# A layer's modulation from transposed weights: products summed along rows on VectorE, gates made into rows by diagonal blocks

## The chip, the cores and the metric

The kernel runs on one core of a Trainium2 chip. Its time is the device time of one execution in microseconds (us); of several runs the median counts. The engines are named TensorE (PE in the profile; PEld is its loading of weights), VectorE (DVE), ScalarE (ACT), GpSimd (POOL) and SyncE (SP), which here only issues DMA transfers.

## The reference

One layer of a decoder trunk over 256 positions of width 2048, all in fp32. What matters here is the modulation: six vectors of 2048 are computed from the conditioning vector `c`, and each half of the layer uses a shift, a scale and a gate.

```python
c_act = jax.nn.silu(c)                                       # (1, 2048)
mod = (c_act @ w_ada[l] + b_ada[l]).reshape(b, N_MOD, 1, d)  # w_ada: 2048 x 12288
shift1, scale1, gate1, shift2, scale2, gate2 = [mod[:, i] for i in range(N_MOD)]
h = rms_norm(x, norm_g[l, 0]) * (1.0 + scale1) + shift1
y = token_mixer(h, ...)             # w_in, three mixers, branch gates, w_out
x = x + gate1 * rms_norm(y, norm_g[l, 1])
h = rms_norm(x, norm_g[l, 2]) * (1.0 + scale2) + shift2
f = jnp.square(jax.nn.relu(h @ w_ff1[l])) @ w_ff2[l]
x = x + gate2 * rms_norm(f, norm_g[l, 3])
```

## The kernel before

**The large products.** h is kept transposed (channels on partitions) as a pair `hhi`, `hlo` whose sum is the fp32 value. Weights come in blocks of 1 MB or less into `raw` (three buffers); `split` (lines 176 to 185) turns a block of 1024 elements a partition into `whi` (a copy on ScalarE, line 183) and `wlo` (the difference on VectorE, line 184), and TensorE multiplies three times for each (lines 203 to 205). `whi` and `wlo` have three buffers each.

**Order of the program.** The start loads x and scales it by its rms, transposes it into `xnT`, and computes the first two columns of shift and scale. Then come five phases over the 16 column blocks of h, in groups of 2, 3, 4, 3 and 4 (`PH`, line 335): in each phase `modulate` (lines 323 to 332) makes h for the group from `a_col` and `t_col`, and 12 chunks of `w_in` are multiplied with it. The columns of the next group are computed between the chunks of a phase. After the phases come attention and the gates of the branches, mixed with one another, then the merge, `w_out`, the second norm, and last the feed-forward part (lines 904 to 931).

**The modulation.** `ada_gemv` (line 265) loads 1 MB or 768 KB of `w_ada` at a time, with its 2048 input rows on the partitions (16 blocks of 128), and adds the block times one column of `sil` (silu of c, a column per block) into `acc` on VectorE (line 281 for the first, line 283 for the rest). What is left is a sum over partitions. `ada_cols` (line 286) takes it on TensorE as matmuls of `acc` with a column of ones (line 292) and adds bias and gain on columns of 16 or fewer elements (lines 296 to 298). `ada_row` (line 300), for the gates, which are needed as rows on all partitions, takes it as matmuls of a matrix of ones with the split `acc` (lines 313, 314) and adds bias and gain (lines 315, 316), which two transfers broadcast from DRAM to all partitions.

**Queues and steps.** These generators are advanced step by step: in the phases by a count in the chunk loop (in the fourth phase, 1.2 steps a chunk, some go to the second half's columns, from `side["ada"]`), later by `fill`, once for each block of four `kt` in `gemm`, at the rate in `side["ada"][1]`. Until the fifth phase the modulation's blocks have three `raw` buffers of their own; from there on (`ring[:] = [st, 3]`, line 696) they share the three of the other weights. All weights are issued on SP's queue in program order: an issue that waits for its buffer holds up those behind it. Within an engine, instructions run in the order that the framework's scheduler gave them.

## Time and profile before

| | before |
|---|---|
| median of 3 runs | 1546.1 us (1539.91 to 1547.72) |
| profiled execution | 1540.46 us, of which 1537.8 us are the span from first to last instruction |
| TensorE busy | 1472.0 us (96%) |
| VectorE busy | 1072.6 us (70%) |
| ScalarE busy | 764.7 us (50%) |
| moved by DMA | 368.61 MB, 240 GB/s on the mean |

[...] In a row of a stretch stand its bounds, its length, the busy time (and the count of instructions) of PE, PEld, DVE, ACT and POOL, then PEclk, the DMA engines' busy share and what they moved. A row of the chain is a piece of the work that ended last: its start, its length and what it was. In a group of instructions the idle time stands in front of what ended it.

### The profile page before, as it was taken

Reading aid. Unit: us, or ns where it says so; the run is one execution under the profiler, and the core shown is the slowest. Engines: PE = TensorE matmul, PEld = TensorE weight load, DVE = VectorE, ACT = ScalarE, POOL = GpSimd, SP = SyncE. Lnnn points to the kernel's source line nnn. Section 1 sums busy time; section 2 is a strip of 40 time slices with the busy share of each in tenths; the row PEclk is TensorE's granted clock in tenths of the full one; section 3 lists DMA queues with packets and bytes.
Section 4 is the critical chain, followed back from the end, with each engine's and each line's share of the span. In section 5 each row is a group of like instructions: output and inputs, shape, how many; then the busy total and the mean of one; then the engine's idle time right before and its main releaser. Section 6 shows DMA issues by size and latency. Waiting matters only on the chain.

```text
span 1537.8 us, 17519 instructions
## 1 busy us (share of the span) xinstructions
PE 1472.0 (96%) x6635; PEld 1193.9 (78%) x6635; DVE 1072.6 (70%) x1358; ACT 764.7 (50%) x1089; POOL 30.0 (2%) x39
## 2 busy tenths in 40 slices
PE   3989999999999999999989999999999999999997
PEld 2768877887777668787867888888888888888886
DVE  6788898778887787779887556666655445454465
ACT  5644334653677765254456453345433544344542
POOL 1000001002000010000000000000000000000000
PEclk8999998998999999999999999999999999999999
DMA  9998988665566668888975667777676555566553
GB/s 321 316 330 302 324 309 302 212 200 180 197 232 212 223 222 316 298 295 294 338 257 174 215 240 246 228 251 241 220 243 216 184 190 191 192 192 192 184 195 113
DMA packets 182339, 368.61 MB, mean 240 GB/s; under 512 B 9722, under 2 KB 22272, under 8 KB 182000
## 3 DMA queue, kind: packets, MB, share of 16 engines
q1 hardware_dynamic: 180640, 363.30, 69.8%
q0 software_dynamic: 1616, 4.20, 0.9%
q8 instruction: 52, 0.85, 0.2%
q14 instruction: 31, 0.25, 0.0%
HBM read 365.38 MB, written 2.10 MB: 239 GB/s over the span
## 4 chain that ended last, share of the span: by engine, by line
PE 83%; DVE 7%; DMA 5%; ACT 2%; issue 1%; SPq 0%; DVEq 0%; ACTq 0%
PE ps_mm L204 25%; PE ps_mm L205 25%; PE ps_mm L203 25%; DVE wlo L184 3%; DVE acc L283 2%; PE ps_x L360 2%; DMA raw<-in_w_ada_dram 2%; ACT whi L183 1%; DMA raw<-in_w_in_dram 1%; PE ps_x L292 1%; DMA raw<-in_w_out_dram 1%; PE ps_x L637 1%; PE ps_x L671 1%; DMA x_h<-in_x_dram 1%; PE ps_pv L663 1%
## 5 line engine op out<-in xcount | busy, mean ns | idle before, releaser
L184 DVE TENSOR_TENSOR wlo<-raw,whi 128x1024 fp32r<-128x1024 f32 x484 | 577.1, 1199 | 373.3 <-ACT whi L183 372.2
L183 ACT ACTIVATE whi<-raw 128x1024 fp32r<-128x1024 f32 x484 | 499.6, 1037 | 606.2 <-PE ps_mm L205 510.7
L204 PE MATMUL ps_mm<-wlo,hhi 128*128 128x512 f32 x1260 | 500.7, 397 | 9.6 <-DVE wlo L184 9.6
L203 PE MATMUL ps_mm<-whi,hhi 128*128 128x512 f32 x1260 | 497.3, 398 | 9.2 <-ACT whi L183 6.1
L205 PE MATMUL ps_mm<-whi,hlo 128*128 128x512 f32 x1260 | 498.7, 396 | 0.0
L204 PEld LDWEIGHTS ps_mm<-wlo,hhi 128*128 128x128 f32 x1260 | 239.6, 190 | 66.3 <-DVE wlo L184 16.7
L203 PEld LDWEIGHTS ps_mm<-whi,hhi 128*128 128x128 f32 x1260 | 238.5, 190 | 61.8 <-ACT whi L183 8.2
L205 PEld LDWEIGHTS ps_mm<-whi,hlo 128*128 128x128 f32 x1260 | 239.3, 190 | 51.4 <-issue 1.9
L283 DVE SCALAR_TENSOR_TENSOR acc<-raw,sil,acc 128x1024 f32<-128x1024 f32 (+2 forms) x195 | 235.2, 1206 | 7.6 <-DMA raw<-in_w_ada_dram 5.3
L203 PE MATMUL ps_mm<-whi,fhi 128*128 128x512 f32 x496 | 193.3, 390 | 0.0
L205 PE MATMUL ps_mm<-whi,flo 128*128 128x512 f32 x496 | 193.0, 389 | 0.0
L204 PE MATMUL ps_mm<-wlo,fhi 128*128 128x512 f32 x496 | 193.0, 389 | 0.0
L205 PEld LDWEIGHTS ps_mm<-whi,flo 128*128 128x128 f32 x496 | 93.1, 188 | 19.3
L204 PEld LDWEIGHTS ps_mm<-wlo,fhi 128*128 128x128 f32 x496 | 93.1, 188 | 19.3
L203 PEld LDWEIGHTS ps_mm<-whi,fhi 128*128 128x128 f32 x496 | 93.1, 188 | 19.2
L643 ACT ACTIVATE e<-e,m 128x128 f32<-128x128 f32 (+1 forms) x64 | 28.3, 443 | 1.9 <-DVE m L640 1.9
L398 DVE TENSOR_TENSOR part<-part,ps_mm 128x512 f32<-128x512 f32 x40 | 25.9, 681 | 4.4 <-PE ps_mm L205 4.4
L909 ACT ACTIVATE r_t<-ps_mm 128x512 f32<-128x512 f32 x32 | 18.8, 589 | 15.7 <-PE ps_mm L205 15.7
L403 DVE TENSOR_TENSOR pl<-ps_x,ph 128x512 fp32r<-128x512 f32 (+1 forms) x32 | 20.9, 675 | 8.1 <-ACT ph L402 8.1
L653 ACT ACTIVATE e<-e,s 128x128 f32<-128x128 f32 (+1 forms) x64 | 23.1, 441 | 5.5 <-DVE s L650 5.5
L204 PE MATMUL ps_mm<-wlo,qe 128*128 128x512 f32 x64 | 25.0, 390 | 0.0
L203 PE MATMUL ps_mm<-whi,qe 128*128 128x512 f32 x64 | 24.9, 392 | 0.0
(283 smaller groups left out, 1060.3 us busy)
## 6 DMA issues: line engine op xcount, KB each, us to landing
raw<-in_w_ff_dram SPq DMA_DIRECT2D x128, 1024.0 KB, 5.2
raw<-in_w_in_dram SPq DMA_DIRECT2D x56, 1024.0 KB, 5.3
raw<-in_w_ada_dram SPq DMA_DIRECT2D x104, 512.0 KB, 5.5
raw<-in_w_ada_dram SPq DMA_DIRECT2D x32, 1024.0 KB, 5.1
raw<-in_w_in_dram SPq DMA_DIRECT2D x24, 768.0 KB, 5.9
raw<-in_w_out_dram SPq DMA_DIRECT2D x16, 1024.0 KB, 5.3
raw<-in_w_ada_dram SPq DMA_DIRECT2D x32, 384.0 KB, 5.8
raw<-in_w_br_nsa_dram SPq DMA_DIRECT2D x8, 1024.0 KB, 5.7
```

Source lines behind the costliest of these rows:

```text
L183: A.activation(hv, v, AF.Copy)
L184: V.tensor_sub(lv, v, hv.bitcast(F32))
L203: T.matmul(outs[t], ahi[:, kt, ts_], hv[:, k, c0:c0 + n], start=f, stop=False, skip_group_check=True)
L204: T.matmul(outs[t], ahi[:, kt, ts_], lv[:, k, c0:c0 + n], start=False, stop=False, skip_group_check=True)
L205: T.matmul(outs[t], alo[:, kt, ts_], hv[:, k, c0:c0 + n], start=False, stop=l, skip_group_check=True)
L283: V.scalar_tensor_tensor(acc, rv[:, :, k], sil[:, kt:kt + 1], acc, ALU.mult, ALU.add)
L360: T.transpose(tb[:, (k * NT + t) * P:(k * NT + t + 1) * P], src[t][:, (k2 * 2 + k) * P:(k2 * 2 + k + 1) * P], ident)
L398: V.tensor_add(d, d, ps)
L403: V.tensor_sub(lo, src, hi.bitcast(F32))
L643: A.activation(e[:, br, 0:L], e[:, br, 0:L], AF.Exp, scale=-1.0, bias=m8[:, hh, br:br + 1], accum_out=s8[:, hh, br:br + 1])
L653: A.activation(es[hh][:, br, 0:L], es[hh][:, br, 0:L], AF.Copy, scale=s8[:, hh, br:br + 1])
L909: A.activation(r_t[:, t], ps[t], AF.Relu)
```

## The change

The host lays `w_ada` out transposed (12288 rows of 2048), so that 128 outputs lie on the partitions and their 2048 inputs along a row; a block of 1 MB is then contiguous in DRAM. `sil` becomes a tile of 128 x 2048, c broadcast to all partitions, with silu computed on all of them (a factor of 0.5 is left to the product). `ada_col` loads a block and gives the 128 sums with one instruction of VectorE, product and sum along the row (`tensor_tensor_reduce`), in place. Nothing is left to sum over partitions. The gates are computed as columns too (`ada_gate`), bias and gain added there; the first gate stands ahead of the second half's columns in the queue of side work. `to_rows` makes rows of them: VectorE multiplies the identity with four columns at a time, giving four diagonal blocks of 128, which are split into two parts and multiplied with the matrix of ones; ScalarE copies the result. The broadcasts of the gates' bias and gain from DRAM go; their columns come through a third small transpose at the start (`rows2`).

```diff
-V_END = 160
+V_G1, V_G3, V_BG1, V_BG2 = 160, 176, 192, 208
+V_END = 224
...
-def trunk_kernel(ctx: ExitStack, tc: tile.TileContext, consts, x, c, norm_g, w_ada, b_ada, w_in,
+def trunk_kernel(ctx: ExitStack, tc: tile.TileContext, consts, w_adaT, x, c, norm_g, b_ada, w_in,
...
     cols = cp.tile([P, V_END], F32, name="cols")
-    sil = cp.tile([P, KT], F32, name="sil")
     a_col = cp.tile([P, KT], F32, name="a_col")
     t_col = cp.tile([P, KT], F32, name="t_col")
+    g1_col = cp.tile([P, KT], F32, name="g1_col")
+    g2_col = cp.tile([P, KT], F32, name="g2_col")
     a2_col = cp.tile([P, KT], F32, name="a2_col")
...
     ring = [pre, 3]
-    crow = pre.tile([KT, P], F32, name="crow")
     rows0 = pre.tile([96, P], F32, name="rows0")
     rows1 = pre.tile([64, P], F32, name="rows1")
-    nc.sync.dma_start(crow, c.rearrange("o (r p) -> (o r) p", p=P))
+    rows2 = pre.tile([64, P], F32, name="rows2")
+
+    sil = ad.tile([P, D], F32, name="sil")
+    for h in range(2):
+        hs = slice(h * 1024, (h + 1) * 1024)
+        nc.sync.dma_start(sil[:, hs], c[0, hs].partition_broadcast(P))
     nc.sync.dma_start(ident, consts[:, C_ID:C_ID + P])
...
         G.dma_start(rows1[k * KT:(k + 1) * KT], bav[sec])
-
-    tp0 = bank("x")
-    T.transpose(tp0[:, 0:KT], crow, ident[0:KT, 0:KT])
-    th = pre.tile([P, 2, KT], F32, name="th")
-    V.tensor_copy(th[:, 0], tp0[:, 0:KT])
-    A.activation(th[:, 1], tp0[:, 0:KT], AF.Tanh, scale=0.5)
-    V.tensor_scalar(th[:, 1], th[:, 1], 0.5, 0.5, ALU.mult, ALU.add)
-    V.tensor_mul(sil, th[:, 0], th[:, 1])
-    A.activation(th[:, 1, 0:1], th[:, 1, 0:1], AF.Sqrt)
+    for k, src in enumerate((norm_g[0, 1], norm_g[0, 3])):
+        G.dma_start(rows2[k * KT:(k + 1) * KT], src.rearrange("(r p) -> r p", p=P))
+    for k, sec in enumerate((2, 5)):
+        G.dma_start(rows2[(k + 2) * KT:(k + 3) * KT], bav[sec])
+
+    for h in range(2):
+        hs = slice(h * 1024, (h + 1) * 1024)
+        th = ring[0].tile([P, 2048], F32, name="raw", tag="raw", bufs=ring[1])[:, 0:1024]
+        A.activation(th, sil[:, hs], AF.Tanh, scale=0.5)
+        V.scalar_tensor_tensor(sil[:, hs], th, 1.0, sil[:, hs], ALU.add, ALU.mult)
+    warm = pre.tile([P, 1], F32, name="warm")
+    A.activation(warm, ident[:, 0:1], AF.Sqrt)
...
         T.transpose(tp1[:, 0:V_POS + 32], rows0[0:V_POS + 32], ident[0:V_POS + 32, 0:V_POS + 32])
-        T.transpose(tp1[:, V_BADA:V_END], rows1, ident[0:64, 0:64])
+        T.transpose(tp1[:, V_BADA:V_BADA + 64], rows1, ident[0:64, 0:64])
+        T.transpose(tp1[:, V_G1:V_END], rows2, ident[0:64, 0:64])
         V.tensor_copy(cols[:, 0:V_POS + 32], tp1[:, 0:V_POS + 32])
...
-    win_v, wada_v = kview(w_in), kview(w_ada)
+    win_v = kview(w_in)
     brp_v, brg_v, brn_v = kview(w_br_pool), kview(w_br_gmlp), kview(w_br_nsa)
...
-    def ada_gemv(c0, c1, acc):
-
-        n = acc.shape[2]
-        nk = 1024 // n
-        for u in range(0, KT, nk):
-            raw = ring[0].tile([P, 2048], F32, name="raw", tag="raw", bufs=ring[1])[:, 0:2 * nk * n]
-            if c1 == c0 + n:
-                rv = raw.rearrange("p (k s n) -> p s k n", k=nk, s=2)
-                nc.sync.dma_start(raw.rearrange("p (k n) -> p k n", k=nk), wada_v[:, u:u + nk, c0:c0 + 2 * n])
-            else:
-                rv = raw.rearrange("p (s k n) -> p s k n", k=nk, s=2)
-                for s_, c_ in enumerate((c0, c1)):
-                    nc.sync.dma_start(rv[:, s_], wada_v[:, u:u + nk, c_:c_ + n])
-            for k in range(nk):
-                kt = u + k
-                if kt == 0:
-                    V.tensor_scalar(acc, rv[:, :, k], sil[:, 0:1], None, ALU.mult)
-                else:
-                    V.scalar_tensor_tensor(acc, rv[:, :, k], sil[:, kt:kt + 1], acc, ALU.mult, ALU.add)
-            yield
+    def ada_col(col, sec, k):
+
+        raw = ring[0].tile([P, 2048], F32, name="raw", tag="raw", bufs=ring[1])
+        r0 = sec * D + k * P
+        nc.sync.dma_start(raw, w_adaT[r0:r0 + P, :])
+        V.tensor_tensor_reduce(raw, raw, sil, 0.5, 0.0, ALU.mult, ALU.add, accum_out=col)
...
-        acc = ad.tile([P, 1024], F32, name="acc", tag="acc", bufs=2)[:, 0:256 * nk]
-        yield from ada_gemv(sec * D + k0 * P, (sec + 1) * D + k0 * P, acc.rearrange("p (s n) -> p s n", s=2))
-        ps = bank("x")
-        for k in range(2 * nk):
-            T.matmul(ps[:, k:k + 1], acc[:, k * P:(k + 1) * P], ones[:, 0:1], start=k == 0, stop=k == 2 * nk - 1,
-                     skip_group_check=True)
+        for k in range(k0, k0 + nk):
+            for s_, c_ in enumerate((t_c, a_c)):
+                ada_col(c_[:, k:k + 1], sec + s_, k)
+                yield
         ks = slice(k0, k0 + nk)
         bs = V_BADA + vsec * KT + k0
-        V.tensor_add(a_c[:, ks], ps[:, nk:2 * nk], cols[:, bs + KT:bs + KT + nk])
+        V.tensor_add(a_c[:, ks], a_c[:, ks], cols[:, bs + KT:bs + KT + nk])
         V.scalar_tensor_tensor(a_c[:, ks], a_c[:, ks], 1.0, cols[:, vg + k0:vg + k0 + nk], ALU.add, ALU.mult)
-        V.tensor_add(t_c[:, ks], ps[:, 0:nk], cols[:, bs:bs + nk])
-
-    def ada_row(n, sec, gi, gg):
-
-        acc = ad.tile([P, 1024], F32, name="acc", tag="acc", bufs=2)
-        c0 = sec * D + n * 1024
-        gs = gg[:, n * 1024:(n + 1) * 1024]
-        nc.sync.dma_start(gs, b_ada[0, c0:c0 + 1024].partition_broadcast(P))
-        yield from ada_gemv(c0, c0 + 512, acc.rearrange("p (s n) -> p s n", s=2))
-        hv, lv = split(acc.rearrange("p (k n) -> p k n", k=2))
-        for b in range(2):
-            ps = bank("pv")
-            bs = slice(b * 512, (b + 1) * 512)
-            gb = ad.tile([P, 512], F32, name="gb", tag="gb", bufs=1)
-            nc.sync.dma_start(gb, norm_g[0, gi, n * 1024 + b * 512:n * 1024 + (b + 1) * 512].partition_broadcast(P))
-            T.matmul(ps, ones_r, hv[:, b], start=True, stop=False)
-            T.matmul(ps, ones_r, lv[:, b], start=False, stop=True)
-            V.tensor_add(gs[:, bs], gs[:, bs], ps)
-            V.tensor_mul(gs[:, bs], gs[:, bs], gb)
+        V.tensor_add(t_c[:, ks], t_c[:, ks], cols[:, bs:bs + nk])
+
+    def ada_gate(sec, vb, vg, g_c):
+
+        for k in range(KT):
+            ada_col(g_c[:, k:k + 1], sec, k)
+            yield
+        V.tensor_add(g_c, g_c, cols[:, vb:vb + KT])
+        V.tensor_mul(g_c, g_c, cols[:, vg:vg + KT])
+        gated.append(sec)
+
+    gated = []
+
+    def to_rows(g_c, gg):
+
+        for n in range(4):
+            dh, dl = (st.tile([P, 1024], F32R, name=t, tag=t, bufs=3)[:, 0:512] for t in ("whi", "wlo"))
+            d32 = st.tile([P, 2048], F32, name="raw", tag="raw", bufs=3)[:, 0:512]
+            V.tensor_tensor(d32.rearrange("p (k n) -> p k n", k=4), ident.unsqueeze(1).broadcast_to([P, 4, P]),
+                            g_c[:, 4 * n:4 * n + 4].unsqueeze(2).broadcast_to([P, 4, P]), ALU.mult)
+            A.activation(dh, d32, AF.Copy)
+            V.tensor_sub(dl, d32, dh.bitcast(F32))
+            ps = bank("x")
+            T.matmul(ps, ones_r, dh, start=True, stop=False)
+            T.matmul(ps, ones_r, dl, start=False, stop=True)
+            A.activation(gg[:, n * 512:(n + 1) * 512], ps, AF.Copy)
+            yield
...
     early_steps = []
+    side["ada"][0].append(ada_gate(2, V_BG1, V_G1, g1_col))
     for kc in range(4):
...
         if ph < NP - 1:
-            nxt, ns = [ada_cols(*PH[ph + 1], 0, 0, V_G0, a_col, t_col)], KT // (8 // PH[ph + 1][1])
+            nxt, ns = [ada_cols(*PH[ph + 1], 0, 0, V_G0, a_col, t_col)], 2 * PH[ph + 1][1]
         order = list(range(NE))[::1 - 2 * ((NP - 1 - ph) % 2)]
...
         T.matmul(pg[0:48, 0:S], lv[:, kt], hhi[:, kt], start=False, stop=kt == KT - 1)
-    gT = ad.tile([48, S], F32, name="gT", tag="gb", bufs=1)
+    gT = t0.tile([48, S], F32, name="gT")
     A.activation(gT, pg[0:48, 0:S], AF.Tanh, scale=0.5)
...
     gg1 = g1p.tile([P, D], F32, name="gg1")
-    rows = []
-
-    def row(n, *args):
-        yield from ada_row(n, *args)
-        rows.append(n)
-
-    side["ada"][0][1:1] = [row(n, 2, 1, gg1) for n in range(2)]
+    while 2 not in gated:
+        step(side["ada"][0])
+    side["rows"] = [[to_rows(g1_col, gg1)], 0.5, 0.0]
...
             ps = gemm_a_last(wout_v, n * 512, act, kept)
-        while n // 2 not in rows:
-            step(side["ada"][0])
+        drain("rows")
         for t in range(NT):
...
     gg2 = fl.tile([P, D], F32, name="gg2")
-    for n in range(2):
-        side["ada"][0].append(ada_row(n, 5, 3, gg2))
+    side["ada"][0] += [ada_gate(5, V_BG2, V_G3, g2_col), to_rows(g2_col, gg2)]
     side["ada"][1] = 0.25
...
-_INS = ['x', 'c', 'norm_g', 'w_ada', 'b_ada', 'w_in', 'pool_w', 'pool_scale', 'gmlp_ln_g', 'gmlp_ln_b',
+def _layouts(inputs):
+
+    import numpy as np
+    laid = {}
+    laid["w_adaT"] = np.ascontiguousarray(inputs["w_ada"][0].T)
+    return laid
+
+
+_INS = ['x', 'c', 'norm_g', 'b_ada', 'w_in', 'pool_w', 'pool_scale', 'gmlp_ln_g', 'gmlp_ln_b',
         'gmlp_ws', 'gmlp_bs', 'cmp_pos', 'cmp_w1', 'cmp_b1', 'cmp_w2', 'cmp_b2', 'w_br_pool', 'w_br_gmlp',
```

What stands in a row of an engine, before and after, at two places. The first is SP's queue at the start, before (`crow` is c as rows, `raw` a block of `w_ada`, `x_h` a half of 128 positions):

```order
L116 DMA crow<-in_c_dram 16x128
L117 DMA cst<-consts_dram 128x128
L277 DMA raw<-in_w_ada_dram 128x4x256 x2
L340 DMA x_h<-in_x_dram 128x1024 x4
L277 DMA raw<-in_w_ada_dram 128x4x256 x6
L173 DMA raw<-in_w_in_dram 128x2x512
```

and of the changed kernel:

```order
L122 DMA sil<-in_c_dram 128x1024 x2
L123 DMA cst<-consts_dram 128x128
L342 DMA x_h<-in_x_dram 128x1024 x2
L279 DMA raw<-in_w_adaT_dram 128x2048
L342 DMA x_h<-in_x_dram 128x1024 x2
L279 DMA raw<-in_w_adaT_dram 128x2048 x3
L183 DMA raw<-in_w_in_dram 128x2x512
```

The broadcast of c, 1 MB as it lands, now stands first, and a block of weights between the halves of x. The second place is VectorE from the end of x's scaling to the first columns of shift and scale, before:

```order
L283 SCALAR_TENSOR_TENSOR acc<-raw,sil,acc 128x512 x8
L148 COPY cols<-ps_x 128x71
L149 COPY cols<-ps_x 128x64
L283 SCALAR_TENSOR_TENSOR acc<-raw,sil,acc 128x512 x4
L184 TENSOR_TENSOR wlo<-raw,whi 128x1024
L296 TENSOR_TENSOR a_col<-ps_x,cols 128x2
L298 TENSOR_TENSOR t_col<-ps_x,cols 128x2
L297 SCALAR_TENSOR_TENSOR a_col<-a_col,cols 128x2
```

and of the changed kernel (ISA is `tensor_tensor_reduce`, its second row the reading of its accumulator):

```order
L280 ISA raw,t_col<-raw,sil 128x2048
L280 ISA t_col 128x1
L158 COPY cols<-ps_x 128x71
L159 COPY cols<-ps_x 128x128
L280 ISA raw,a_col<-raw,sil 128x2048
L280 ISA a_col 128x1
L292 TENSOR_TENSOR t_col<-t_col,cols 128x2
L290 TENSOR_TENSOR a_col<-a_col,cols 128x2
L194 TENSOR_TENSOR wlo<-raw,whi 128x1024
L291 SCALAR_TENSOR_TENSOR a_col<-a_col,cols 128x2
```

Between the two copies of `cols` and `a_col` four multiply-adds and a round through TensorE (line 292 of before) became one long instruction, and a `wlo` moved ahead of the last operation on `a_col`. In the loop of the phases the two multiply-adds of a step mostly stand together before, and one `ISA` pair takes their place.

## Rows read from the trace of the kernel before

**Rows 1.** The page, the chain that ended last: shares of the span by line.
```profile
PE ps_mm L204 25%; PE ps_mm L205 25%; PE ps_mm L203 25%; DVE wlo L184 3%; DVE acc L283 2%; PE ps_x L360 2%; DMA raw<-in_w_ada_dram 2%; ACT whi L183 1%; DMA raw<-in_w_in_dram 1%; PE ps_x L292 1%; DMA raw<-in_w_out_dram 1%; PE ps_x L637 1%; PE ps_x L671 1%; DMA x_h<-in_x_dram 1%; PE ps_pv L663 1%
```

**Rows 2.** Stretches: bounds, length, busy time of five engines, PEclk, DMA share, GB/s.
```profile
0.00:34.00 34.00, 9.98 (x46) 7.62 (x46) 20.65 (x43) 19.56 (x31) 6.54 (x17) 0.92 0.97 324
...
60.00:260.00 200.00, 189.02 (x826) 152.84 (x825) 175.73 (x205) 86.63 (x107) 0.00 (x0) 0.97 0.91 317
...
400.00:600.00 200.00, 199.11 (x877) 144.64 (x876) 163.31 (x320) 139.75 (x316) 7.08 (x4) 1.00 0.67 232
600.00:800.00 200.00, 194.02 (x861) 158.19 (x860) 162.27 (x173) 89.84 (x115) 0.00 (x0) 0.98 0.87 304
800.00:1538.00 738.00, 719.10 (x3241) 595.78 (x3239) 422.81 (x426) 339.18 (x399) 0.00 (x0) 0.99 0.62 206
```

**Rows 3.** The chain in order of time: start, length, what, xcount.
```profile
4.79 9.40 DMA x_h<-in_x_dram
...
28.24 1.65 PE ps_x L292 x8
...
63.90 1.25 PE ps_x L292 x12
...
120.06 1.92 PE ps_x L292 x16
189.67 1.23 PE ps_x L292 x12
...
232.31 2.23 PE ps_x L292 x16
...
397.19 1.68 PE ps_x L292 x16
...
619.15 5.27 DMA raw<-in_w_ada_dram
624.60 7.62 DMA raw<-in_w_in_dram
```

**Rows 4.** Line 283 by stretch: bounds, length, VectorE's busy time (xcount), PEclk, DMA.
```profile
60.00:260.00 200.00, 65.17 (x56) 0.97 0.91 317
...
400.00:600.00 200.00, 45.56 (x35) 1.00 0.67 232
600.00:800.00 200.00, 52.52 (x41) 0.98 0.87 304
```

**Rows 5.** Groups by form: line, engine, op, tiles, shapes, xcount, busy us, mean ns.
```profile
L283 DVE SCALAR_TENSOR_TENSOR acc<-raw,sil,acc 128x1024 f32<-128x1024 f32 x150 | 193.5, 1290 | 6.3 <-DMA raw<-in_w_ada_dram 4.8
...
L283 DVE SCALAR_TENSOR_TENSOR acc<-raw,sil,acc 128x768 f32<-128x768 f32 x30 | 30.4, 1014 | 0.3
...
L640 DVE CUSTOM_DVE_ANT_0 e<-ps_x,cst 128x256 f32<-128x256 f32 x32 | 11.8, 420 | 1.4 <-PE ps_x L637 1.3
L283 DVE SCALAR_TENSOR_TENSOR acc<-raw,sil,acc 128x512 f32<-128x512 f32 x15 | 11.3, 751 | 0.9 <-DMA raw<-in_w_ada_dram 0.4
...
L640 DVE CUSTOM_DVE_ANT_0 e<-ps_x,cst 128x128 f32<-128x128 f32 x32 | 7.8, 287 | 1.7 <-PE ps_x L637 1.5
...
L640 DVE DVE_READ_ACCUMULATOR2_ANT m<- 128x1 f32 x64 | 5.3, 83 | 0.0
```

**Rows 6.** Timeline before the first matmul: start, length, engine, line, op, tiles.
```profile
24.99 3.10 DVE L283 SCALAR_TENSOR_TENSOR acc<-raw,sil,acc 128x512 f32<-128x512 f32 x4
28.01 1.22 DVE L184 TENSOR_TENSOR wlo<-raw,whi 128x1024 fp32r<-128x1024 f32 x1
...
30.36 1.09 ACT L330 ACTIVATE h<-xnT,t_col,a_col 128x256 f32<-128x256 f32 x2 [4.51 <-DVE a_col L297]
...
32.30 0.61 ACT L331 ACTIVATE hhi<-h 128x512 fp32r<-128x512 f32 x1
```

**Rows 7.** DMA issues: tiles, queue, xcount, size of one, median us to landing.
```profile
gb<-in_norm_g_dram SPq DMA_DIRECT2D x8, 256.0 KB, 5.3
gg<-in_b_ada_dram SPq DMA_DIRECT2D x4, 512.0 KB, 6.3
```

More of the change, by code (lines that the diff above doesn't have):

```diff
@@ L984 @@
     args.append(nc.dram_tensor("consts_dram", cst.shape, _mybir.dt.float32, kind="ExternalInput").ap())
+    for name, a in _layouts(inputs).items():
+        arrays[f"in_{name}_dram"] = a
+        args.append(nc.dram_tensor(f"in_{name}_dram", a.shape, _mybir.dt.from_np(a.dtype), kind="ExternalInput").ap())
     for name in _INS:
```

## The prediction

> **What bounds the kernel now.** I read the chain first, then the stretches, then the chain again in order of time. The chain that ended last is TensorE's matmuls of lines 203 to 205 for three quarters of the span, VectorE's `wlo` and `acc` for 5%, transfers of weights for 4% [rows 1]. So the first question for every edit is whether it takes work off TensorE, and the second whether it moves one of the places where TensorE waits. The table of stretches shows those places [rows 2]. From 800 us on (most of it the feed-forward part, where TensorE is only idle at both ends) and from 400 to 600 us (attention and gates, 0.9 us idle) TensorE has no time to lose. Idle time stands in three places: the first 34 us (24 us idle: nothing can start before the first columns of h exist), 60 to 260 us (11 us idle), and 600 to 800 us (6 us idle). The reader should look at the other columns of these two rows. In 60 to 260 VectorE is busy for 175.7 of 200 us and the DMA engines for 0.91: both are near their end, and TensorE's 11 idle us come from them. In 600 to 800 the DMA share is 0.87, and the chain there runs through two transfers that TensorE stood waiting for, 5.3 and 7.6 us long [rows 3].
>
> The modulation's share of this: its multiply-adds take 65.2 us of VectorE's time in 60 to 260, 45.6 in 400 to 600 and 52.5 in 600 to 800 [rows 4], and the sums over partitions, one-column matmuls, stand on TensorE in nine short runs [rows 3].
>
> **Part by part, what is removed.** The nine runs of line 292 go. Their pieces of the chain are 1.65 us (start), 1.25, 1.92, 1.23 and 2.23 (60 to 260) and four of 1.68 (397, 490, 585 and 653 us; one is shown, the others read alike) [rows 3]: 15.0 us of a full TensorE. How much of it comes back depends on what ends last there, so I take them by stretch below. The partition sums of the gate rows (lines 313, 314) are replaced by as many matmuls of the same size on the diagonal blocks: 16 against 16, nothing.
>
> **VectorE.** Before, 1 MB of weights costs two multiply-adds of 1290 ns, 2.58 us (in the steps with 384 columns it is 768 elements, 1014 ns each, 16 for what is now six steps) [rows 5]. After, it costs one product-and-sum of 2048 elements, and no such instruction is in the trace. The nearest row is the same form in attention: 287 ns for 128 elements and 420 for 256 [rows 5], that is 1.04 ns an element, so 287 + 1920 x 1.04 = 2.28 us. Its accumulator read follows, 83 ns, which needs no more than that. The other bound is that the rate differs because both operands now lie in SBUF, where attention reads one from PSUM; the multiply-add, which reads two fp32 tiles from SBUF, gains 539 ns for 512 more elements, 1.05 ns each [rows 5], the same rate. I take 2.28. In 60 to 260 the loop's steps are 27 now (8, 6, 8 and about 5 early ones), 61.6 us against 65.2 of line 283 [rows 4] and a few first products on line 281 beside it: 4 to 6 us less on an engine that has 24 to spare there. What queues behind the long instruction is the next `wlo`, 2.28 us where it was 1.29; but two multiply-adds mostly stood together before (order, in the section on the change), so the block does not grow.
>
> **The start.** The last half of x lands at 14.19 us (4.79 + 9.40) [rows 3]. The last four multiply-adds begin at 24.99 and take 3.10; h begins at 30.36 and takes 1.09; `hhi` begins at 32.30, 0.85 us after h, with a `whi` between them [rows 6]. Now SP issues 1 MB of `sil`, then half of x, then 1 MB of weights, then the second half of x: ahead of the last half of x stand 1 MB more bytes than before. At the stretch's 324 GB/s [rows 2] that is 3.2 us, with the whole chain of rms, scaling, transposes and columns behind it; it is nothing if landing and not bandwidth sets the time. I take 2.9, near the upper end, since the DMA share is 0.97 there. Behind it: one product of 2.28 for the 3.10, no 1.65 us on TensorE, but in the new order a `wlo` (1.22 us [rows 6]) stands ahead of the last operation on `a_col`, and no `whi` stands between h and `hhi`. Sum: +2.9 - 0.8 - 1.65 + 1.2 - 0.85 = +0.8. Bounds: -2.1 without the first term, and +3. I take +1.
>
> **60 to 260 us.** 6.6 us of TensorE work go (1.25 + 1.92 + 1.23 + 2.23), VectorE loses 4 to 6, and 27 MB come in one issue a step in place of two, which I do not count as a gain. If VectorE alone set this stretch, it still shrinks by what VectorE loses; if all idle time went too, by 6.6 + 11 = 17.6. The low end, 3, is a stretch where only the sections without idle time pay (120 and 190 us). I take 8.
>
> **320 to 600 us.** Three runs of 1.68 us on a TensorE with no idle time between 400 and 600, and little before: 5.0 us, bounds 4 and 6.
>
> **600 to 800 us.** One run of 1.68 goes. The gate's bias and gain rows, broadcast to all partitions, go as well: half of 4 x 512 KB and 8 x 256 KB [rows 7] belongs here, 2 MB, at 304 GB/s [rows 2] 6.9 us of transfers in a stretch that waits for transfers. Against it, the four diagonal blocks of the first gate take one of three `raw` buffers each, and one `whi` and one `wlo`, on the way from product to copy to difference, behind other work of VectorE and ScalarE, while TensorE's next matmuls in order wait for them; a buffer out of use for some microseconds can bring a wait like one of the two in [rows 3] back. Between 0 and 9 us gained I take 5. The second gate's blocks lie after 800 us, where the DMA share is 0.62 and VectorE has 315 us to spare [rows 2]: nothing.
>
> **Sum.** +1 - 8 - 5 - 5 = -17 against the profiled execution's 1540.46 us (span 1537.8 and 2.7 around it): 1523.5. That execution lies 5.6 us under the median of the three runs and 0.5 above the lowest, so a median of a few runs may come as high as 1529. I forecast **1525**, and 1515 to 1533 for this case alone.
>
> **The rivals.** (a) *The sum along rows runs at half rate.* The operands are two fp32 tiles in SBUF, and an accumulator beside them; the trace has no such instruction. At 2.08 ns an element a step would take 4.41 us. 60 to 260 us: 27 steps cost 119 us, 51 more than now; VectorE then needs 227 us for what is done in 200, and at today's share (88%) 258, so 27 to 58 us longer; 400 to 600 (18 steps, 34 more): 0 to 41; 600 to 800 (21 steps, 40 more): 2 to 50. Less the 15 of TensorE that is 1555 to 1675, about 1615. It decides from some 2.9 us a step on: a step takes 2.5 now, and 27 x 0.4 eats the 10 us won elsewhere. Against it stands that line 283 reads two fp32 tiles from SBUF at 1.05 ns [rows 5].
>
> [...]
>
> (b) *The removed matmuls were in the shade.* Where VectorE or a transfer ends last, TensorE's 10 us outside attention turn into idle time, and the start loses 1: 1540.5 - 5 + 1 = 1536.5. For it speaks VectorE's 88%; against it that VectorE loses as much, and that most of 60 to 260 has TensorE at 189 of 200.
>
> (c) *The idle time goes too*: -2 (start), -17.6, -5, -9: 1507. For it speaks that two waits are for transfers that shrink; against it that the buffers, not bytes alone, set when a transfer starts.
>
> (d) *The diagonal blocks bring waits*: four like the two in [rows 3], 5.3 to 7.6 us each, are 21 to 30 us; with the other terms as they are 1540.5 + 1 - 8 - 5 - 2 + 26 = 1552. It decides from 14 us in all on. For it speaks that the stretch waits for transfers now; against it that the copies of `raw` wait for VectorE only briefly there (TensorE idles 6 us in 200).
>
> **How the numbers follow.** The forecast gets 0.62, (a) 0.08, (b) 0.15, (c) 0.10, (d) 0.05. Faster by over 0.5% (8 us, about what a measurement of this kernel can tell from no change) are the forecast nearly whole and (c): 0.73. Within 0.5% is (b) and the forecast's tail: 0.15. Slower: (a), (d): 0.12. The range reaches from (c) to (b) with the 5.6 us of the median on top, 1508 to 1542; it leaves out (a) and (d).
>
> **What would show it.** In the profile after: no one-column matmuls; the product-and-sum of 2048 elements at 2.2 to 2.4 us (at 4.4 rival (a) holds); the first matmul of line 213 at 32 to 36 us; VectorE's busy time some 20 us lower; 400 to 600 us of before done in 5 less; TensorE's idle time between 60 and 260 not above 11. I am wrong in size if the start slips by more than 3 us or if the stretch around the first diagonal blocks shows new waits of `ps_x` for VectorE; wrong in kind if VectorE comes out above 1100 us.

## The result, and the profile of the changed kernel

The changed kernel takes 1521.32 us (median of 4 runs, 1519.10 to 1524.53), the kernel before 1543.01 us beside it (4 runs, 1538.42 to 1547.72): a ratio of 0.9871, 95% interval 0.9846 to 0.9897, so 1.3% faster. The forecast was 1525.

First the page of the profiled execution (1522.03 us): its span, busy times and packets.

```profile
span 1519.7 us, 17069 instructions
PE 1451.0 (95%) x6507; PEld 1173.1 (77%) x6507; DVE 1052.1 (69%) x1341; ACT 770.4 (51%) x1102; POOL 36.4 (2%) x43
DMA packets 147074, 365.47 MB, mean 241 GB/s; under 512 B 8458, under 2 KB 8768, under 8 KB 134448
```

VectorE has 20.5 us less work than before (1072.6), TensorE 21.0 (1472.0). The groups of instructions show the new operations: the product-and-sum, its accumulator read, and the three steps of a diagonal block on VectorE and ScalarE (count | busy us, mean ns | idle before).

```profile
L280 DVE CUSTOM_DVE_ANT_0 raw<-raw,sil 128x2048 f32<-128x2048 f32 x96 | 219.2, 2286 | 9.3 <-DMA raw<-in_w_adaT_dram 9.3
L310 DVE TENSOR_TENSOR raw<-cst,g_col 128x512 f32<-128x512 f32 x8 | 5.5, 692 | 0.2
L313 DVE TENSOR_TENSOR wlo<-raw,whi 128x512 fp32r<-128x512 f32 x8 | 5.5, 691 | 4.7 <-ACT whi L312 4.7
L312 ACT ACTIVATE whi<-raw 128x512 fp32r<-128x512 f32 x8 | 5.1, 632 | 16.0 <-PE ps_mm L215 10.0 <-DVE t_col L292 6.0
L280 DVE DVE_READ_ACCUMULATOR2_ANT t_col<- 128x1 f32 x32 | 2.7, 84 | 0.0
```

The stretches, with the columns of [rows 2] (PEclk is the granted clock of TensorE as a share of its full clock):

```profile
60.00:260.00 200.00, 188.15 (x798) 150.36 (x797) 179.19 (x208) 89.56 (x110) 4.73 (x8) 0.98 0.90 334
400.00:600.00 200.00, 199.49 (x868) 146.12 (x867) 161.09 (x305) 139.14 (x311) 11.58 (x4) 1.00 0.70 245
600.00:800.00 200.00, 183.96 (x805) 147.79 (x804) 162.11 (x201) 95.05 (x134) 0.00 (x0) 0.97 0.77 273
800.00:1538.00 738.00, 710.53 (x3201) 589.33 (x3199) 401.98 (x391) 329.36 (x380) 0.00 (x0) 0.99 0.61 201
```

Equal windows of two kernels hold different work once one is ahead, so I follow the weights' matmuls themselves (lines 203 to 205, now 213 to 215; 5760 in each kernel). The table has the start of the n-th, in us, read from the trace; the experiments' rows are used below. Number 865 is near the end of the columns' stretch, 1825 near the end of attention, 2785 just behind the start of the feed-forward part. Other work can lie on either side of a number: behind 1825, attention's own matmuls and transposes still hold 2.7 us of TensorE before, 6.2 in the changed kernel (in both of its profiled executions; the second stands beside an experiment below) and nothing in the layout alone.

| kernel | 1 | 865 | 1153 | 1825 | 2209 | 2785 | 5760 |
|---|---|---|---|---|---|---|---|
| before | 32.97 | 258.18 | 338.29 | 582.24 | 683.64 | 836.90 | 1527.93 |
| changed | 34.03 | 252.67 | 332.73 | 563.47 | 668.06 | 819.49 | 1510.14 |
| ones' round put back | 33.67 | 255.12 | 335.40 | 572.00 | 679.74 | 833.19 | 1523.84 |
| layout alone | 33.99 | 257.08 | 337.09 | 582.70 | 676.73 | 831.35 | 1522.35 |
| own tiles | 34.00 | 252.18 | 332.21 | 562.95 | 660.11 | 813.49 | 1504.28 |
| x first | 32.94 | 249.58 | 329.95 | 562.67 | 667.90 | 820.08 | 1510.73 |
| sum short | 31.03 | 247.13 | 327.06 | 563.88 | 660.26 | 809.78 | 1500.43 |
| sum and load short | 31.51 | 229.91 | 309.90 | 544.92 | 636.32 | 785.06 | 1475.72 |
| sum twice | 38.37 | 293.86 | 386.01 | 649.71 | 769.25 | 937.06 | 1627.92 |

Changed less before: +1.1 at the first matmul, -6.6 more to 865, nothing to 1153, **-13.2** to 1825, **+1.4** to 2785, -0.4 behind it. The total is what I forecast; two of its terms are not. Of the -13.2 some 3.5 us are attention's work that now lies behind number 1825, and they stand in the +1.4 again. In the second profiled execution of the changed kernel the terms are +0.6, -7.2, -0.2, -14.3, +3.8 and -0.4, with the same total: two executions place a few microseconds differently.

In the start, the chain of work in order of time (start us, us, what) has a product of VectorE between two scalings of x, the transposes of x on TensorE, then VectorE's last product, and the `wlo` that the order put ahead of the last operation on `a_col`:

```profile
15.27 2.20 DVE raw L280
...
19.47 2.19 ACT x_h L355 x2
22.26 3.79 PE ps_x L362 x16
28.08 0.23 DVE cols L158
28.51 2.20 DVE raw L280
30.83 1.23 DVE wlo L194
32.22 1.10 ACT h L332 x2
33.34 0.64 ACT hhi L333
34.03 0.79 PE ps_mm L213
```

From 600 to 668 us, where three of the first gate's four blocks stand, the same chain runs through three transfers that TensorE stood waiting for. Before, it had two in this part [rows 3].

```profile
613.76 0.61 DVE wlo L313
614.41 0.51 PE ps_x L316
...
623.82 5.01 DMA raw<-in_w_in_dram
...
652.95 7.26 DMA raw<-in_w_in_dram
...
663.80 7.80 DMA raw<-in_w_br_nsa_dram
```

**The clock's part of a time.** Executions of one kernel differ by more than I knew: 45 of the kernel before, beside the experiments, took 1533.9 to 1551.5 us. They follow the mean granted clock of TensorE: at 0.977 the median is 1549.6, at 0.980 1543.2, at 0.984 1539.5, and the one at 0.988 took 1533.9. Taking one minus the clock, times the span, from each time leaves 1514.3 us with a standard deviation of 2.0, where the times themselves have 4.7. I use this "time less the clock's part" beside the time; it is an upper bound of what the clock took, since some half-clock pieces hold idle time (from 804 to 810 us of the kernel before TensorE is busy for 0.07 of 6.00 us, at a granted 0.50). By it the kernel before stands at 1514.3 (clock 0.983) and the changed one at 1503.9 (0.988, 10 executions): of some 18 us, at least 10 are work and waits, and at most 8 go with a higher clock.

### The profile page after: what moved, and what is told of

Its sections match the earlier page's. It is cut to its first block, busy times and chain, and to the rows that moved or that the text cites. A ratio compares the mean times of both kernels' runs of the same rounds, so it can differ in the third digit from the quotient of the medians.

```text
span 1519.7 us, 17069 instructions
## 1 busy us (share of the span) xinstructions
PE 1451.0 (95%) x6507; PEld 1173.1 (77%) x6507; DVE 1052.1 (69%) x1341; ACT 770.4 (51%) x1102; POOL 36.4 (2%) x43
## 4 chain that ended last, share of the span: by engine, by line
PE 80%; DVE 10%; DMA 4%; ACT 3%; issue 2%; POOL 0%; DVEq 0%; ACTq 0%; POOLq 0%
PE ps_mm L214 25%; PE ps_mm L215 25%; PE ps_mm L213 24%; DVE wlo L194 4%; DVE raw L280 3%; PE ps_x L362 2%; ACT whi L193 1%; DMA raw<-in_w_in_dram 1%; DMA raw<-in_w_adaT_dram 1%; PE ps_x L639 1%; PE ps_x L673 1%; DVE part L400 1%; PE ps_pv L665 1%; PE ps_pv L664 1%; DMA raw<-in_w_br_nsa_dram 1%
## 5 line engine op out<-in xcount | busy, mean ns | idle before, releaser
L280 DVE CUSTOM_DVE_ANT_0 raw<-raw,sil 128x2048 f32<-128x2048 f32 x96 | 219.2, 2286 | 9.3 <-DMA raw<-in_w_adaT_dram 9.3
L906 ACT ACTIVATE r_t<-ps_mm 128x512 f32<-128x512 f32 x32 | 18.8, 588 | 15.7 <-PE ps_mm L215 15.7
L362 PE MATMUL ps_x<-cst,x_h 128*128 128x128 f32 x32 | 7.3, 400 | 20.1 <-DVE x_h L353 15.3
```

The lines of the kernel that those rows point to most:

```text
L280: V.tensor_tensor_reduce(raw, raw, sil, 0.5, 0.0, ALU.mult, ALU.add, accum_out=col)
L362: T.transpose(tb[:, (k * NT + t) * P:(k * NT + t + 1) * P], src[t][:, (k2 * 2 + k) * P:(k2 * 2 + k + 1) * P], ident)
L906: A.activation(r_t[:, t], ps[t], AF.Relu)
```

## Experiments

**The sums' round put back.** Does the TensorE work that was removed pay?

```
+        ps = bank("x")
+        for k in range(2 * nk):
+            c_ = (t_c, a_c)[k // nk]
+            T.matmul(ps[:, k:k + 1], ident, c_[:, k0 + k % nk:k0 + k % nk + 1], start=k == 0, stop=k == 2 * nk - 1,
+                     skip_group_check=True)
...
-        V.tensor_add(a_c[:, ks], a_c[:, ks], cols[:, bs + KT:bs + KT + nk])
+        V.tensor_add(a_c[:, ks], ps[:, nk:2 * nk], cols[:, bs + KT:bs + KT + nk])
...
-        V.tensor_add(t_c[:, ks], t_c[:, ks], cols[:, bs:bs + nk])
+        V.tensor_add(t_c[:, ks], ps[:, 0:nk], cols[:, bs:bs + nk])
```

> The changed kernel with the sums' round through TensorE put back: at the end of each group of columns, 2 one-column matmuls of the identity for each new column of t and a (64 in all) into a bank of PSUM, and the two additions read that bank; nothing else differs. My theory (the removed TensorE work pays nearly whole, the sum along rows pays little): 9 to 15 us over the changed kernel's 1521, so 1530 to 1536, with 4 to 7 of it in 60 to 260 us and 3 to 5 in 320 to 600 us. Rival (b), that the removed matmuls lay in the shade outside attention: at most 5 us, 1522 to 1527, and the milestones at 60 to 260 us where the changed kernel has them.

Measured: 1534.9 us (12 runs, 1532.17 to 1538.52), ratio to before 0.9950 (0.9927 to 0.9974), so some 13 us over the changed kernel; less the clock's part 1512.2, 8 over it. The total is what I expected; its parts are not. By the table: -0.4 at the first matmul, then +2.8 to number 865, 5.9 from 1153 to 1825, 3.2 from there to 2209, 2.0 to 2785. The put-back runs of 16 stand at 581, 641 and 715 us, the fourth in two parts at 746 and 773; they hold 7.4 us of TensorE, and the stretches with them lose 5.2 (2.8 against the second profiled execution of the changed kernel). Those between 34 and 228 us hold 7.4 us too and cost 2.8 (3.4 against the second). The 5.9 us were a surprise: no put-back matmul stands between 228 and 580 us. The stretches from 350 to 370 us say what it is. In the kernel before:

```profile
350.00:360.00 10.00, 6.42 (x35) 5.30 (x34) 9.91 (x21) 4.54 (x9) 3.46 (x2) 0.98 0.76 268
360.00:370.00 10.00, 10.00 (x36) 8.76 (x36) 5.66 (x20) 1.88 (x4) 1.83 (x2) 0.51 0.58 186
```

In this kernel:

```profile
350.00:360.00 10.00, 7.20 (x31) 6.04 (x30) 8.96 (x24) 3.20 (x6) 3.48 (x2) 0.77 0.64 230
360.00:370.00 10.00, 10.00 (x41) 8.80 (x41) 5.58 (x19) 1.87 (x4) 1.79 (x2) 0.55 0.43 140
```

In the changed kernel:

```profile
350.00:360.00 10.00, 8.37 (x52) 7.02 (x52) 8.89 (x31) 1.89 (x5) 2.69 (x3) 1.00 0.60 205
360.00:370.00 10.00, 9.65 (x70) 8.51 (x70) 7.21 (x13) 2.97 (x5) 1.44 (x2) 1.00 0.61 217
```

TensorE waits there for attention's compression in all three. In the first two it is idle for some 3 us in one piece (3.6 and 2.8), and then runs at half clock for 10.2 us before and 13.7 in this kernel, with 36 and 41 matmuls in a slice (0.51 and 0.55 granted) that holds 70 in the changed one (1.00). In the changed kernel the idle time is in two parts (2.4 and 1.0), and the clock stays full. Half of 13.7 us is 6.8, so the clock can account for all of the 5.9. The ones' work stands elsewhere; that it brings the piece by shifting the moments at which things meet is my reading, not shown.

**Layout alone.** The kernel before with its own arithmetic, the weights in blocks on the host.

```
-            if c1 == c0 + n:
-                rv = raw.rearrange("p (k s n) -> p s k n", k=nk, s=2)
-                nc.sync.dma_start(raw.rearrange("p (k n) -> p k n", k=nk), wada_v[:, u:u + nk, c0:c0 + 2 * n])
-            else:
-                rv = raw.rearrange("p (s k n) -> p s k n", k=nk, s=2)
-                for s_, c_ in enumerate((c0, c1)):
-                    nc.sync.dma_start(rv[:, s_], wada_v[:, u:u + nk, c_:c_ + n])
+            rv = raw.rearrange("p (s k n) -> p s k n", k=nk, s=2)
+            r0 = BLOCKS[c0, c1, n][u // nk] * P
+            nc.sync.dma_start(raw, w_adaB[r0:r0 + P, 0:2 * nk * n])
```

> The kernel before with its own arithmetic (two multiply-adds a step, one-column sums on TensorE, gate rows by ones and bias rows by broadcast), but the modulation weights laid out in blocks of 1 MB (768 KB where the step has 384 columns), one contiguous transfer a step in place of two of 256 or 512 columns; only the transfers differ. My theory (the matmuls and VectorE's work carry the gain, the transfers of 60 to 260 us are not what paces): 0 to 5 us under the kernel before, 1538 to 1543. Rival, the longer pieces of the transfers carry it (the DMA engines are 0.91 busy in 60 to 260 us, and the packets fall from 182339 to 147074): 8 to 20 us under it, 1523 to 1535, most of it before 260 us and from 600 to 710.

Measured: 1534.45 us (12 runs), ratio 0.9962 (0.9937 to 0.9987); less the clock's part 1511.5. So 5 to 6 us with the clock's part, at my bound and under the rival's, and 2.8 without it. In the profiled execution it comes to 2.1 us between numbers 1 and 865 and to 6.0 from 1825 to 2785, and neither can be given to the transfers. At half clock the first stretch spends 16.0 us before and 10.1 here, up to 3.0 us of time. Of the 6.0, 2.7 are attention's work and 1.7 a run of 16 one-column matmuls, which here stand ahead of number 1825 (the stretch up to it is 1.7 longer than before), and up to 3.4 are a piece of 6.8 us at half clock that stands at 632.6 us in the kernel before and not here.

**The diagonal blocks in tiles of their own, whole and in halves.**

```
-            dh, dl = (st.tile([P, 1024], F32R, name=t, tag=t, bufs=3)[:, 0:512] for t in ("whi", "wlo"))
-            d32 = st.tile([P, 2048], F32, name="raw", tag="raw", bufs=3)[:, 0:512]
+            dh, dl = (g1p.tile([P, 512], F32R, name=t, tag=t, bufs=1) for t in ("dh", "dl"))
+            d32 = g1p.tile([P, 512], F32, name="d32", tag="d32", bufs=1)
```

> The changed kernel with the diagonal blocks (the product, its copy, the difference) in three tiles of their own in place of one buffer each of the raw, whi and wlo rings. Theory: the 4 us lost between 600 and 710 us come from the blocks holding ring buffers, so that weights' loads and halves wait; then 3 to 6 us come back there, 1515 to 1518, by the milestones of that stretch. Rival: the stretch is paced by transfers and by the half-clock piece at 616.7 us, whatever buffers the blocks use; then 0 +- 1.5 us, about 1521.

Measured: 1514.97 us (6 runs), ratio 0.9827 (0.9788 to 0.9867). The changed kernel and this one again, side by side on another chip:

> The changed kernel as it is, beside the next run on one chip. Over 34 executions of the kernel before, the time less what the mean granted clock took (one minus the clock, times the span) was 1514 us with little spread, and by the same reckoning the changed kernel stood at 1504 and own tiles at 1498.5. Expected: 1520 to 1524 in all, 1502 to 1506 less the clock's part.

> The changed kernel with the diagonal blocks in tiles of their own, once more, beside the changed kernel on one chip. If the 6.8 us between the two ratios of the earlier runs hold: 1513 to 1518, with 1497 to 1500 less the clock's part, 4 to 7 us under the run beside it. If that difference was one of chips: within 2 us of the run beside it.

Measured: 1521.71 (0.9886, 0.9856 to 0.9915) and 1515.31 us (0.9844, 0.9821 to 0.9868), 6 runs each; less the clock's part 1503.8 and 1499.8. The 6 us hold, and the table puts 7.4 of them between numbers 1825 and 2209. Of the chain from 600 to 668 us, by lines, transfers are 30% in the changed kernel:

```profile
by line: DMA raw<-in_w_in_dram 18.1%; PE ps_mm L214 15.4%; DVE wlo L194 14.3%; PE ps_mm L215 13.4%; DMA raw<-in_w_br_nsa_dram 11.5%; PE ps_mm L213 10.3%; ACT whi L193 7.7%; issue 3.6%; DVE raw L280 2.4%; DVE gt L810 2.1%; ACT gt L761 1.1%; 
```

With own tiles it holds none:

```profile
by line: PE ps_mm L214 30.9%; PE ps_mm L215 30.5%; PE ps_mm L213 29.8%; PE ps_x L362 2.6%; DVE gt L810 1.9%; DVE wlo L194 1.8%; DVE mab L811 1.1%; issue 0.8%; PE ps_x L316 0.7%; PE ps_x L315 0.3%; DVEq L810 0.0%
```

VectorE's timeline of the changed kernel shows how long a block keeps a `raw` buffer. The third one's product is written at 618.91, and its difference, the last reader, comes 7.0 us later, behind two `wlo`, a wait and a product-and-sum; for the other three it is 6.5, 2.1 and 5.8 us.

```profile
618.91 0.69 DVE L310 TENSOR_TENSOR raw<-cst,g_col 128x512 f32<-128x512 f32 x1
619.52 1.22 DVE L194 TENSOR_TENSOR wlo<-raw,whi 128x1024 fp32r<-128x1024 f32 x1
622.57 1.22 DVE L194 TENSOR_TENSOR wlo<-raw,whi 128x1024 fp32r<-128x1024 f32 x1 [1.82 <-ACT whi L193]
623.71 2.28 DVE L280 CUSTOM_DVE_ANT_0 raw<-raw,sil 128x2048 f32<-128x2048 f32 x1
625.92 0.08 DVE L280 DVE_READ_ACCUMULATOR2_ANT a_col<- 128x1 f32 x1
625.92 0.69 DVE L313 TENSOR_TENSOR wlo<-raw,whi 128x512 fp32r<-128x512 f32 x1
```

Two kernels part the edit: `d32` alone in a tile of its own, and `dh` and `dl` alone.

> The changed kernel with only the product of the diagonal blocks in a tile of its own (the raw ring keeps its three buffers for weights); the two halves still take a slot each of the whi and wlo rings. If the raw buffer is what cost 600 to 660 us its 7 us (the loads of w_in and the modulation wait for a buffer that holds a product of 512 columns until its difference is done): 4 to 7 us under the changed kernel, as with own tiles for all. If the halves' slots are (the next block's whi and wlo wait until TensorE is through with the diagonal block): within 2 us of the changed kernel.

> The complement: the two halves of a diagonal block in tiles of their own, its product still in a buffer of the raw ring. If the raw buffer is the cause: within 2 us of the changed kernel; if the halves' slots are: 4 to 7 us under it. If both give about half, each slot costs by itself.

Measured: 1517.92 and 1520.61 us (5 runs each), ratios 0.9864 (0.9833 to 0.9896) and 0.9875 (0.9847 to 0.9903); less the clock's part 1500.9 and 1501.7, against 1503.9 with neither and 1499.1 with both (12 executions). From number 1825 to 2209 they take 100.9 and 101.6 us, where the changed kernel takes 104.6 and 105.9 in its two profiled executions and own tiles 97.2 in both. Transfers hold 15.2 and 13.6 us of the chain from 580 to 670 us, as against 20.1 in the changed kernel and none with own tiles. So either kind of slot costs something there. In the totals the parts are too small to be told from each other, and the second gives its lead back by number 2785 (820.99): its chain there runs through seven transfers of `w_out`, the changed kernel's through one; why, no run shows.

**x first, alone and with own tiles.**

```
+    for t in range(NT):
+        for h in range(2):
+            nc.sync.dma_start(x_h[t][h], xv[:, t, h * 1024:(h + 1) * 1024])
     for h in range(2):
         hs = slice(h * 1024, (h + 1) * 1024)
         nc.sync.dma_start(sil[:, hs], c[0, hs].partition_broadcast(P))
...
-    for t in range(NT):
-        for h in range(2):
-            nc.sync.dma_start(x_h[t][h], xv[:, t, h * 1024:(h + 1) * 1024])
```

> The changed kernel with the four loads of x issued ahead of the two halves of silu's input, which moves nothing else by hand. The first matmul of line 213 stands at 34.0 us, and what ends last ahead of it is the second half of x at 15.7 us and the rms, scaling, transposes and columns behind it. If x's landing sets the start, x comes 3 to 6 us earlier and the first matmul at 28 to 31 us, 1516 to 1519 in all. Rival: the first columns wait as long for the product-and-sum (silu's input and the first blocks of weights now land later, and VectorE does the four products then): the first matmul at 33 to 36 us, 1520 to 1524.

> The changed kernel with both edits: the diagonal blocks in tiles of their own and x's loads first. With own tiles alone the profiled span fell by 5.8 us; with x first alone the milestones stood 3.1 us earlier from 84 to 330 us and only 0.7 us earlier from 397 us on, after the wait around 350 us and a half-clock piece at 376. Theory: what is won at the start is given back around 350 to 397 us whatever comes after, so 5 to 8 us under the changed kernel, about own tiles alone. Rival: x first lost its 3 us by where a half-clock piece happened to fall; then 8 to 11 us under it.

Measured: 1523.31 us (6 runs, 0.9880, 0.9841 to 0.9919) alone, 1515.85 (4 runs, 0.9841, 0.9810 to 0.9872) with own tiles: no gain in either. The last part of x is in work at 10.9 us in place of 15.7, but the first matmul stands at 32.94, because now VectorE's products stand in the chain of work (x first alone):

```profile
20.05 2.29 DVE raw L283
23.48 2.20 DVE raw L283
26.03 2.20 DVE raw L283
28.43 2.20 DVE raw L283
31.13 1.10 ACT h L335 x2
```

The 3 us that the table shows at number 865 are gone by number 1345 (397.00 against 397.67): a half-clock piece of 6.8 us stands at 374.6 (0.73 and 0.93 granted from 370 to 390 us), where the changed kernel has none (1.00).

**What the columns' stretch waits for.** The sum over 256 of the 2048 elements; then the load cut to these too.

```
-        V.tensor_tensor_reduce(raw, raw, sil, 0.5, 0.0, ALU.mult, ALU.add, accum_out=col)
+        V.tensor_tensor_reduce(raw[:, 0:256], raw[:, 0:256], sil[:, 0:256], 0.5, 0.0, ALU.mult, ALU.add, accum_out=col)
```

and in the second kernel also

```
-        nc.sync.dma_start(raw, w_adaT[r0:r0 + P, :])
+        nc.sync.dma_start(raw[:, 0:256], w_adaT[r0:r0 + P, 0:256])
```

> The changed kernel with the product-and-sum over the first 256 of a block's 2048 elements, so that it costs VectorE some 0.42 us in place of 2.29 (the modulation's values are then not the reference's); every transfer stays. It tells what TensorE's 11.8 idle us between 60 and 260 us and the shade of the put-back matmuls there wait for. If VectorE: 60 to 260 us ends 8 to 12 us earlier, 1505 to 1513 in all. If the transfers (0.90 busy there): 0 to 4 us earlier, 1516 to 1521.

> The same with the transfers cut too: of each block of 1 MB only the 256 columns that are summed are loaded. If the transfers are what 60 to 260 us waits for: 60 to 260 us ends 8 to 12 us earlier than in the changed kernel, and the run is 6 to 12 us under the one with the short sum alone. If VectorE is: within 3 us of the short sum alone.

Measured: 1511.26 (4 runs) and 1489.95 us (4 runs). The stretch from 60 to 260 us with the short sum:

```profile
60.00:260.00 200.00, 189.07 (x810) 151.72 (x809) 130.96 (x208) 88.87 (x109) 4.72 (x8) 0.99 0.91 334
```

and with the short load too:

```profile
60.00:260.00 200.00, 199.61 (x892) 165.22 (x891) 129.81 (x173) 92.73 (x113) 5.62 (x9) 1.00 0.65 209
```

With 48 us of VectorE's work gone, TensorE is idle for 10.9 us as against 11.8, at the same 334 GB/s; with the transfers cut it is idle for 0.4. TensorE's waits in this stretch (us in total, times, longest) name VectorE's `wlo`, in the changed kernel:

```profile
PE ps_mm L214 <- DVE wlo L194: 10.7, 11, 3.0
```

With the short sum they do so still:

```profile
PE ps_mm L214 <- DVE wlo L194: 9.1, 9, 1.6
```

The name is only the last link, since VectorE itself waits there for `whi`, and ScalarE, which makes it, mostly for TensorE and little for a landing:

```profile
DVE wlo L194 <- ACT whi L193: 56.0, 49, 4.0
ACT whi L193 <- PE ps_mm L215: 79.6, 47, 3.5
ACT whi L193 <- DMA raw<-in_w_in_dram: 4.6, 3, 2.3
```

The waits go round in a ring of engines and do not name the transfers; the run with the short load does. Between numbers 1 and 865 the short sum gains 2.5 us, the short load 20.2. So the transfers hold this stretch near its length even without VectorE's products. Whether the whole sum would hold it too once the transfers are short was not run. The expectation for the short load was too small. In total the short sum came out where I expected it if VectorE set the stretch (10 us under the changed kernel), but only 2.5 of that lie in it: 3.0 are won in the start and 4.1 from 1153 to 2785.

**The sum done twice.**

```
         V.tensor_tensor_reduce(raw, raw, sil, 0.5, 0.0, ALU.mult, ALU.add, accum_out=col)
+        V.tensor_tensor_reduce(raw, raw, sil, 0.5, 0.0, ALU.mult, ALU.add, accum_out=spare)
```

> The changed kernel with each product-and-sum done twice (the second into a spare column and read by nobody), so that a step of 1 MB costs VectorE 4.57 us, about what rival (a) of the prediction priced (4.41). By the sum of the prediction for rival (a): 29 to 149 us over the changed kernel, some 75 to 90, of it 27 to 58 in 60 to 260 us and 0 to 41 in 400 to 600. If VectorE's own limit were not what the columns' stretch waits for: under 20 us in all.

Measured: 1639.76 us (one run), 118 over the changed kernel, at a clock of 0.962; less the clock's part 1577.5, 74 over it. That is inside the wide range and above the 75 to 90. The new line costs 220.1 us of VectorE. By the table the loss is 4.3 us at the first matmul, 36.9 from 1 to 865, 12.1 from there to 1153, 33.0 from 1153 to 1825, 31.3 from there to 2785. The new line's group of instructions:

```profile
L282 DVE CUSTOM_DVE_ANT_0 raw<-raw,sil 128x2048 f32<-128x2048 f32 x96 | 220.1, 2293 | 0.5
```

And its stretch from 60 to 260 us, in which VectorE is busy for 196 of 200 us and TensorE idle for 31:

```profile
60.00:260.00 200.00, 168.55 (x701) 135.86 (x700) 195.88 (x214) 78.83 (x96) 0.00 (x0) 0.93 0.80 278
```

## Why the prediction held in sum, and where its steps failed

**VectorE's price: right.** 2.28 us forecast, 2.286 measured. Rival (a) falls. It took half the rate of 1.04 ns an element, 4.41 us a step, an assumption that no row showed; 2048 fp32 elements with accumulation take 2286 ns, 1.1 ns an element (256 take 429 ns in the short sum, so each further one 1.04). The multiply-add before, from two tiles and without accumulation, took 1.05 for each further one [rows 5]. In the changed kernel a scaling with one SBUF tile as its source takes 0.53 ns an element (269 ns for 512 more), about half of either:

```profile
L353 DVE TENSOR_SCALAR x_h<-x_h,r_r 128x1024 f32<-128x1024 f32 x2 | 1.5, 750 | 0.0
L875 DVE TENSOR_SCALAR z<-x,r_r 128x512 f32<-128x512 f32 x8 | 3.4, 481 | 0.1
```

The sum done twice lies in the bounds which I put on the rival: 27 to 58, 0 to 41 and 2 to 50 us by stretch, measured 37, 33 and 31 in the nearest stretches of the table. These bounds leave out the start and 260 to 340 us, 16 us more, and the clock, which is up to 45 of the 118.

**The start: +1 forecast, +1.1 measured (+0.6 in the second execution), by other parts than I gave.** I gave x's later landing 2.9 us; the last part of x is in work 1.5 us later (15.7 against 14.2), and a product of 2.20 us that stands between two scalings of x I had not counted. Bringing x 4.8 us earlier gave back 1.1, since VectorE's products then end last; shortening the products alone gave 3.0. The two lie within some 2 us of each other.

**60 to 260 us: -8 forecast, -6.6 measured, with the wrong cause.** I let VectorE and TensorE share the limit, and gave the transfers nothing. They hold the stretch: the short sum leaves TensorE's idle time, the short load takes it away. The 6.6 us of matmuls removed there paid some 2.8, as the put-back shows, so rival (b)'s mechanism holds for more than half of them; and the idle time, forecast at no more than 11 us, is 11.8. Up to 1.7 more is the clock's (16.0 us at half clock before, 12.7 after). The remaining 2.1 us no run parts further.

**320 to 600 us: -5 forecast, -13.2 measured from number 1153 to 1825: the term that was mis-sized.** Three parts add up to it. Two of the three runs of 1.68 us stand ahead of number 1825, 3.4 (the third, at 585 us, stands behind it). Some 3.5 are attention's work, which is not saved but now lies behind the number. And the kernel before spends 10.2 + 3.4 us at half clock at 360 and 390 us, behind a wait of attention, and the changed kernel none, which is up to 13.6 / 2 = 6.8. With the third run counted here and attention's work left out, the term is -11.4 (-12.5 in the second execution). That the clock belongs to this sum I had not considered. With the ones' round put back the piece returned, with x first a part of it; what decides whether it comes is left open. The length of the idle time ahead of it does not settle it: 2.4 and 1.0 us stand ahead of none in the changed kernel, 1.9 (from 340 to 350 us) ahead of some 3.4 us at half clock (370 to 390 us, 0.84 and 0.99 granted) in the kernel with own tiles.

**600 to 800 us: -5 forecast, +1.4 measured from 1825 to 2785, -0.4 (+2.0 in the second execution) by the same two corrections: the step that failed.** Gains were there: the run at 653 us is gone, and 3.4 us are spent at half clock where it was 6.8, up to 1.7 us of time. But I set the blocks' hold on the buffers too low ("for some microseconds", "a buffer out of use ... can bring a wait ... back"). Rival (d)'s mechanism was right, at 6 us, not at 21 to 30. TensorE's idle time from 1825 to 2209 is 3.5 us before, 5.1 in the changed kernel and 1.5 with own tiles. With own tiles the stretch from 1825 to 2785 takes 250.5 us against 254.7 before (256.0 in the changed kernel), a gain of 4.1; in the second execution it is 5.6. By the two corrections that is 5.9 and 7.4: the -5 of the forecast with the waits taken out, and up to 3.4 of it is again the clock's, since own tiles have no piece at half clock from 1825 to 2209.

**Behind 800 us: nothing forecast, -0.4 measured.** The sum, +1.1 - 6.6 - 13.2 + 1.4 - 0.4 = -17.8, meets the forecast by luck: a clock that I had left out (up to 7 us of gain) and the buffers (6 us of loss) are of one size.

## What to carry to other kernels

A small tile borrowed from a ring costs the time until its last reader is done, not its own few instructions: here 2 to 7 us of one in three buffers, four times, with a slot of each of the halves' rings, were worth 6 us, and 6 KB a partition for tiles of its own gave them back (1515 us, 1.6 to 1.7% under the kernel before). A wait that names an engine does not show that the engine sets the pace: VectorE was named, cutting 48 us of its work left the wait, and cutting the transfers as well took it away. A number that marks a place in the program is checked for the other work on either side of it: 3.5 us of attention moved across one here. And where executions differ, the mean granted clock goes beside each time before a few microseconds are given to a cause.

## What the runs showed of the hardware

A wait of TensorE cost more than its length where the clock fell behind it: 3.6 us idle at 350 to 360 us in the kernel before, then 10.2 us at half clock, in which most chain pieces of one matmul take 0.43 us, against 0.23 at full clock; in the changed kernel 2.4 us idle were followed by no half clock. With the sum done twice the clock's mean is 0.962 against 0.988, and up to 45 of 118 us are its part. And the product-and-sum sits at a knee: 2.29 us a step more costs 118 us (one run), 1.86 less gives back 10. Of VectorE's instructions on fp32, the scaling from one tile took 0.53 ns for each further element (481 ns for 512, 750 for 1024), the multiply-add from two 1.05 (751 for 512, 1290 for 1024) and the product-and-sum from two 1.04 (429 for 256, 2286 for 2048).
